# Four blocks of a second matrix asked for on GpSimd's queue, a hand order over a second norm, and two gates ahead of a late split

## The chip, the cores and the metric

The kernel runs on one core of one Trainium2 chip. Its engines are TensorE (PE in the rows, its weight loads PEld), VectorE (DVE), ScalarE (ACT), GpSimd (POOL) and SyncE (SP); each works through its own instructions in order, and DMA transfers are issued on a queue of SyncE or of GpSimd. The metric is the device time of one execution in microseconds, as the median of several runs. Where a time is given with two decimals and no unit, it is microseconds from the start of the profiled span.

## The reference

A decoder of two layers over 512 tokens of width 1024, in float32. Layer 0 mixes by pooling, layer 1 by a gated unit (SGU); both have an MLP of width 4096 behind it. Every matrix is applied in float32 accuracy.

```python
def sgu_mixer(h, w_in, ln_g, ln_b, w_s, b_s, w_out):
    z = jax.nn.gelu(h @ w_in, approximate=False)
    u, v = jnp.split(z, 2, axis=-1)
    v = layernorm(v, ln_g, ln_b)
    ...
    mixed = jnp.einsum('hts,bnshc->bnthc', ws, v) + b_s.T[None, None, :, :, None]
    gated = u * mixed.reshape(B_, S_, SGU_WIDTH)
    return gated @ w_out

def sq_relu_mlp(h, w1, w2):
    return jnp.square(jax.nn.relu(h @ w1)) @ w2

for i in range(DEPTH):
    mod = c_act @ ada_w[i] + ada_b[i]
    sh1, sc1, g1, sh2, sc2, g2 = jnp.split(mod, 6, axis=-1)
    h = modulate(rmsnorm(x, norm_mix_g[i]), sh1, sc1)
    y = pool_mixer(...) if i == 0 else sgu_mixer(...)
    x = x + g1[:, None, :] * y
    h = modulate(rmsnorm(x, norm_mlp_g[i]), sh2, sc2)
    x = x + g2[:, None, :] * sq_relu_mlp(h, mlp_w1[i], mlp_w2[i])
return rmsnorm(x, final_g)
```

## The kernel before, in words

**Products.** A float32 product is made of three products of rounded halves (`mm3`): a weight is split into `wh` (ScalarE, L199, in the SGU L1245) and `wl`, the rest (VectorE, L200, L1251), an activation into `hb` or `o` in the same way (L678, L679; L1399, L1403). So each block of 128 by 1024 weights passes ScalarE and then VectorE before TensorE can use it, and there are a few buffers for the split pairs.

**Units.** The big matrices are multiplied by a scheme with seven products of block sums in place of eight, after Strassen. A unit carries the number m of its product, in the order 1, 5, 6, then 3, 7, 2 and last 4. For m = 1, 5, 6, 4 the weight sums are made in memory, in one tile for each block: it holds the block of one product, is split, and then a DMA on GpSimd's queue adds the next block onto it (`accum_op=ALU.add`; L953 for M2, L820 for M1, L1281 for the SGU's `u`). So each such add waits for the low split (VectorE) of the product before, and the next split waits for the add. M1 is the first matrix of the MLP, M2 the second: its units (c, m) have c = 0 to 3. M2's `bt` tiles serve m = 1, 5, 6, 4, its `b` tiles m = 3 and 7; `b_load` fills the `b` tiles of c = 0 and 1 ahead and an add then turns the blocks of m = 3 into those of m = 7.

**SGU.** `u_run(j, m)` is TensorE's part of the unit (j, m) of the SGU's `u`; `u_hi`, `u_lo` are its splits, `u_add` the adds, `u_out` the eviction of its result. (1, 7) adds onto the bank of (1, 6) once `u_out(1, 6)` has copied it, (1, 4) comes last. `mix(h)`, `gate(h)`, `low(h)` are, for head h, the product with the spatial weights, the product with `u` and its high half, and the low half.

**Second norm.** Layer 1's MLP begins with a norm of the residual `x`, whose token tiles 0 and 1 make the first half and tiles 2 and 3 the second. Each tile's residual is added (VectorE, L1102, L1103), its squares are summed (ScalarE, L1113), the root is taken (VectorE L1126, then a power on GpSimd, L1127), `xs` is the scaled tile (L1153), and TensorE transposes it (`px`, L1166). `spill` writes a pair of tiles of `x` to memory (`xd`, L270), after which their buffer takes loads of MLP blocks, `raws` among them (L805).

**Order.** TensorE's order is always written by hand. VectorE, ScalarE, SyncE and GpSimd follow the hand order in some stretches (the SGU and the first half of the second norm among them); elsewhere a scheduler orders them at compile time by priority and by its own due times. `tc.keep_in_program_order` pins one instruction where it is written.

Of the kernel before, what the change touches and what calls it, by code (L numbers as in the profile page):

```python
# [14 lines left out]
P = 128  # L15
D = 1024
# [71 lines left out]
def decoder_kernel(ctx: ExitStack, tc: tile.TileContext, xtok, vecs, rows, fgrow, ada0, adag, ada1, pool_w, w1s, w1f, w1b, w2, w_v, w_u, w_o, wsT, wsN, lnp, bs, out):  # L88
# [624 lines left out]
    def mlp(i, extra, units, final):  # L713
# [105 lines left out]
        def more_of(u, o, r, n):  # L819
            G.dma_start(o, w1b[i, 2 * u[0] + u[1], r, n], accum_op=ALU.add)  # L820

        def s_sum(u):
            c, j, m = u
            if m in (5, 6) and u not in summed:
                summed.add(u)
                t = blk(c, j, 0, 0)
                if (i, m) == (1, 5) and c < 2:
                    more_of(u, t, *CHAIN[m])
                else:
                    V.tensor_tensor(t, t, blk(c, j, *CHAIN[m]), ALU.add)  # L830
                if m == 5:
                    more_of(u, blk(c, j, 0, 1), 1, 1)
# [84 lines left out]
        def b_load(c):  # L917
            t = slot(XT[c % 2], [P, 2, D], "b")
            b2[c] = [t[:, q] for q in range(2)]
            for q in range(2):  # L920
                nc.sync.dma_start(b2[c][q], piece(c, 1, 1, q))
# [271 lines left out]
    def p_units(*sums):  # L1193

        us = [("p", (c, m)) for m in (1, 5, 6) for c in range(4)]
        us += [("p", u) for u in ((0, 3), (1, 3), (1, 2), (0, 7), (1, 7), (2, 3), (3, 3), (2, 2), (2, 7), (3, 7), (3, 2))]
        us.insert(5, ("p", (0, 2)))
        after(us, ("p", (1, 6)), ("bl", (0,)), ("bl", (1,)))
        us += [("p", (c, 4)) for c in range(4)]
        after(us, ("p", (2, 2)), ("xl", (0,)))  # L1200
        after(us, ("p", (2, 7)), ("xl", (1,)))
        after(us, ("p", (3, 7)), ("sum", (0, 1)), ("sum", (1, 1)))
        for at, t, dh in sums:
            after(us, ("p", at), ("sum", (t, dh)))
        return us
# [314 lines left out]
    us += p_units(((3, 2), 0, 0), ((3, 2), 1, 0), ((1, 4), 2, 1), ((1, 4), 3, 1))  # L1520
# [149 lines left out]
    u_hi(1, 5)  # L1670
    u_run(0, 3)
    u_lo(1, 5)
    u_add(ub[0][:, 1], 1, 1, 1)
# [3 lines left out]
    u_lo(0, 4)  # L1677
    u_hi(1, 2)
    gate(2)
    gate(3)  # L1680
    u_run(1, 1)
# [4 lines left out]
    u_hi(1, 6)  # L1686
    u_lo(1, 2)
    u_lo(1, 6)
    u_run(0, 4)
    u_hi(1, 3)  # L1690
    column(24)
    gate(0)
    gate(1)
    low(0)
    low(1)
    for q in (28, 29):
        c_load(q, f"T2{q % 2}")
# [93 lines left out]
    v1 = sm.tile([P, 2], F32, name="rv", tag="rv2")  # L1791
    r1 = sm.tile([P, 2], F32, name="rr", tag="rr2")
    xs_ = slot("R0", [P, 2, D], "xs")

    def root(q):
        s = sums[0][0][:, q]
        V.scalar_tensor_tensor(v1[:, q : q + 1], s[:, 0:1], RMS_EPS, s[:, 1:2], ALU.add, ALU.add)
        G.tensor_tensor(r1[:, q : q + 1], v1[:, q : q + 1], mhalf[:, 0:1], ALU.pow)

    def first_half():  # L1800
        h32[:] = [slot(f"P{j}", [P, 4, S], "h32") for j in range(2)]
        h_[:] = hparts(["S0", "S1", "S2", "S3"])
        for k in range(0, KD, 2):
            turn_cols(0, k, (xs_[:, 0], xs_[:, 1]))
        for ks in ((0, 2), (4, 6)):
            for k in ks:
                modulate(0, k, 1)
            for k in ks:
                hi(tts[k])
            for k in ks:  # L1810
                lo(tts[k])

    for t in range(NT):
        pos[t] = bank("po", xz)
        for n, k in enumerate(ks_):
            if (t, n) == (3, 2):
                first_half()
                by[0].__exit__(None, None, None)
                spill(0)
            mm3(pos[t], cut(gt[k], ALL, tok[t]), cut(w_["o", 1, k // 2], ALL, slice(S * (k % 2), S * (k % 2) + S)), k == 2, k == 5)  # L1820
        with tc.high_priority():
            gated(t, S, S, pos[t])
        if t == 0:
            root(0)
            columns_(38)
            A.activation(xs_[:, 0], X(0), AF.Copy, scale=r1[:, 0:1])
        elif t == 1:
            root(1)
            columns_(39)
            sums.pop(0)  # L1830
            A.activation(xs_[:, 1, 0:S], X(1)[:, 0:S], AF.Copy, scale=r1[:, 1:2])
            V.tensor_scalar(xs_[:, 1, S:D], X(1)[:, S:D], r1[:, 1:2], None, ALU.mult)
# [54 lines left out]
    halves_ = normed_parts(1, 1, 1, None, True)  # L1887

    def second():
        with tc.high_priority():  # L1890
            next(halves_)
        spill(1)

    def second_too():
        with tc.high_priority():
            next(halves_, None)
# [92 lines left out]
```

## Time and profile before

| | |
|---|---|
| time, median of 3 runs | 834.9 us (834.65 to 835.15) |
| the profiled execution | 834.98 us, with a span of 833.3 us |
| mean granted clock of TensorE | 0.994 |
| TensorE busy | 820.6 us, 98% of the span |
| VectorE, ScalarE, GpSimd busy | 83%, 63%, 14% |
| moved by DMA | 194.94 MB, mean 234 GB/s |

The span is the time from the first to the last recorded instruction of the profiled execution; 1.7 us lie around it. The busy shares are averages over stages in which different things are awaited.

### The profile page before, as it was taken

To read this page: it belongs to the slowest core of one execution; us is meant where nothing else is said; L and a number is where in the kernel's file an instruction comes from. 1 tells how busy PE (TensorE), PEld (TensorE's weight loads), DVE (VectorE), ACT (ScalarE), POOL (GpSimd) and SP (SyncE) were. 2 spreads that over 40 slices of the span, in tenths; PEclk is the share of its full clock that TensorE was granted. 3 is DMA by queue.
4 is the path that set the end of the run, shared out by engine and by line. 5 is a ranking of instruction groups with operands and counts; after the bars stand their busy time and mean duration, and the time that the engine had idled before them with its cause. 6 is when DMAs were issued, how large, how long until landed. Compare 5 with 4: busy or idle time off the path is not lost.

```text
span 833.3 us, 13029 instructions
## 1 busy us (share of the span) xinstructions
PE 820.6 (98%) x5012; PEld 729.6 (88%) x5012; DVE 693.1 (83%) x885; ACT 526.2 (63%) x759; POOL 120.1 (14%) x149
## 2 busy tenths in 40 slices
PE   9999999999999999999999999999999999999996
PEld 6878899999888888888899889999999988888885
DVE  6999999998789868798979887795887578976887
ACT  3286787866756655667565436886766776655662
POOL 3010010000223210000311003101001032321000
PEclk8999999999999999999999999999999999999999
DMA  9999879999999989365797899965887699998502
GB/s 358 407 369 334 301 160 289 282 285 267 278 227 191 207 231 249 122 227 199 228 250 184 271 301 300 258 182 123 253 255 205 199 218 242 190 214 228 170 7 95
DMA packets 53620, 194.94 MB, mean 234 GB/s; under 512 B 6163, under 2 KB 6323, under 8 KB 52534
## 3 DMA queue, kind: packets, MB, share of 16 engines
q1 hardware_dynamic: 37296, 133.98, 44.4%
q0 software_dynamic: 15968, 59.79, 37.2%
q8 instruction: 39, 0.64, 0.3%
q10 hardware_dynamic: 294, 0.34, 0.1%
q14 instruction: 23, 0.19, 0.1%
HBM read 187.79 MB, written 6.31 MB: 233 GB/s over the span
## 4 chain that ended last, share of the span: by engine, by line
PE 62%; DVE 17%; DMA 12%; ACT 4%; issue 4%; POOL 1%; POOLq 0%; ACTq 0%; DVEq 0%; SPq 0%
PE pm L996 27%; PE po L212 7%; DMA ada<-in_ada 6%; DVE wl L200 4%; PE b305q L996 2%; PE b315q L996 2%; DMA bt<-in_w 2%; PE b211q L212 2%; ACT wh L199 2%; PE b311q L212 1%; PE b111q L212 1%; PE b101q L212 1%; PE b301q L212 1%; PE b201q L212 1%; DVE ada L424 1%
## 5 line engine op out<-in xcount | busy, mean ns | idle before, releaser
L996 PE MATMUL pm<-wh,o 128*128 128x512 f32 x736 | 182.5, 390 | 0.6 <-DVE o L679 0.6
L996 PEld LDWEIGHTS pm<-wh,o 128*128 128x128 f32 x736 | 137.7, 188 | 29.6 <-DVE o L679 1.1
L996 PE MATMUL pm<-wl,o 128*128 128x512 f32 x368 | 98.4, 389 | 0.0
L199 ACT ACTIVATE wh<-bt 128x1024 fp32r<-128x1024 f32 x62 | 64.8, 1058 | 45.0 <-PE pm L996 33.6
L200 DVE TENSOR_TENSOR wl<-bt,wh 128x1024 fp32r<-128x1024 f32 x62 | 75.1, 1219 | 15.3 <-ACT wh L199 15.2
L996 PEld LDWEIGHTS pm<-wl,o 128*128 128x128 f32 x368 | 69.1, 188 | 14.4
L679 DVE TENSOR_TENSOR o<-g,o 128x1024 fp32r<-128x1024 f32 x55 | 67.0, 1218 | 6.2 <-ACT o L678 6.2
L678 ACT ACTIVATE o<-g 128x1024 fp32r<-128x1024 f32 x55 | 57.5, 1047 | 10.1 <-PE pm L996 7.2
L199 ACT ACTIVATE wh<-b 128x1024 fp32r<-128x1024 f32 x32 | 34.0, 1063 | 37.6 <-PE pm L996 31.4
L953 POOL DMA_DIRECT2D bt<-in_w x48 | 41.8, 900 | 107.4 <-DVE wl L200 103.7
L200 DVE TENSOR_TENSOR wl<-b,wh 128x1024 fp32r<-128x1024 f32 x32 | 39.2, 1224 | 21.3 <-ACT wh L199 21.3
L212 PE MATMUL po<-hb,wh 128*128 128x256 f32 (+1 forms) x176 | 41.7, 329 | 0.0
L735 ACT ACTIVATE g<-g 128x512 f32<-128x512 f32 (+1 forms) x72 | 40.5, 579 | 1.1
L212 PE MATMUL po<-wh,gt 128*128 128x512 f32 x128 | 40.7, 395 | 0.0
L212 PE MATMUL po<-wh,hb 128*128 128x512 f32 x128 | 40.7, 396 | 0.0
L236 DVE SCALAR_TENSOR_TENSOR ada<-ada,cb 128x1024 f32<-128x1024 f32 x32 | 39.0, 1218 | 0.7 <-DMA ada<-in_ada 0.7
L1113 ACT ACTIVATE tmp<-x 128x512 f32<-128x512 f32 (+1 forms) x24 | 14.9, 621 | 31.9 <-DVE x L1103 31.8
L212 PEld LDWEIGHTS po<-hb,wh 128*128 128x128 f32 x176 | 29.7, 188 | 3.2
L199 ACT ACTIVATE wh<-raw 128x1024 fp32r<-128x1024 f32 x19 | 20.2, 1062 | 16.6 <-PE pm L996 13.5
L200 DVE TENSOR_TENSOR wl<-raw,wh 128x1024 fp32r<-128x1024 f32 x19 | 23.1, 1220 | 8.8 <-ACT wh L199 8.8
L1265 DVE SCALAR_TENSOR_TENSOR ada<-ada,cb 128x1024 f32<-128x1024 f32 x24 | 29.1, 1217 | 1.6 <-DMA ada<-in_ada 1.6
L212 PE MATMUL po<-hb,wl 128*128 128x256 f32 (+1 forms) x88 | 29.2, 332 | 0.0
(532 smaller groups left out, 2281.4 us busy)
## 6 DMA issues: line engine op xcount, KB each, us to landing
ada<-in_ada SPq DMA_DIRECT2D x74, 512.0 KB, 5.5
bt<-in_w POOLq DMA_DIRECT2D x48, 512.0 KB, 10.4
bt<-in_w SPq DMA_DIRECT2D x16, 512.0 KB, 6.3
raw<-in_w SPq DMA_DIRECT2D x16, 512.0 KB, 7.0
b<-in_w SPq DMA_DIRECT2D x16, 512.0 KB, 4.8
b<-in_w POOLq DMA_DIRECT2D x16, 512.0 KB, 10.2
wh<-in_ada SPq DMA_DIRECT2D x8, 512.0 KB, 9.4
wl<-in_ada SPq DMA_DIRECT2D x8, 512.0 KB, 10.0
```

The costliest lines, as they stand in the source:

```text
L199: A.activation(h[:, c], r[:, c], AF.Copy)
L200: V.tensor_tensor(l[:, c], r[:, c], f32(h[:, c]), ALU.subtract)
L212: T.matmul(o[:, c], a, b[:, c], start=first and q == 0 and not c.start, stop=last and q == 2 and c.stop is None, **kw)
L236: keep(V.scalar_tensor_tensor(r, r, 1.0, cb, ALU.mult, ALU.mult, accum_out=pmv[i, b][:, j : j + 1]))
L424: V.scalar_tensor_tensor(r, r, 1.0, cb, ALU.mult, ALU.mult, accum_out=out)
L678: A.activation(o[0], a, AF.Copy)
L679: V.tensor_tensor(o[1], a, f32(o[0]), ALU.subtract)
L735: A.activation(t, t, AF.Square)
L953: G.dma_start(r, piece(c, *nxt, q), accum_op=ALU.add)
L996: T.matmul(banks[hf], o[a][:, 2 * q + p, hf], w[q][b][:, S * p : S * p + S], start=start and q + n + p == 0, stop=stop and q + n + p == 4, ...
L1113: A.activation(tmp, xt, AF.Square, scale=D**-0.5, accum_out=o)
L1265: V.scalar_tensor_tensor(r, r, 1.0, cb, ALU.mult, ALU.mult, accum_out=pm[:, n : n + 1])
```

## The change

There are three parts. TensorE's order of instructions is the same in both kernels; only the other engines' and the queues' order differs.

In **layer 0's M2**, the four plain loads of the `b` tiles for c = 0 and 1 leave SyncE's queue for GpSimd's, and they are pinned in program order, behind unit (1, 5). One add of M1 (layer 1, first block column, m = 5) is pinned in program order too.

In **layer 1's second norm**, the second half was a generator that the scheduler ordered (`normed_parts`). Now its steps are written into the hand order: `residual`, `square_`, `root` and `scaled` of tile 2 between the steps of the first half, and those of tile 3 after it. `xs` of tile 3 is made in two halves, one by ScalarE and one by VectorE. `spill(0)` is written earlier, `spill(1)` at the end; the hand order ends only then.

In the **SGU's u blocks**, the splits of (1, 5), and with them the add that makes (1, 6), stand behind `gate(2)` and `gate(3)`; those of (1, 6) behind `gate(0)`, `gate(1)`, `low(0)` and `low(1)`; the high split of (1, 3) is last.

```diff
-                    more_of(u, blk(c, j, 0, 1), 1, 1)
+                    o = blk(c, j, 0, 1)
+                    if (i, c) == (1, 0):
+                        tc.keep_in_program_order(more_of(u, o, 1, 1))
+                    else:
+                        more_of(u, o, 1, 1)
 
         def s_prep(u):
...
             for q in range(2):
-                nc.sync.dma_start(b2[c][q], piece(c, 1, 1, q))
+                if i == 0 and c < 2:
+                    tc.keep_in_program_order(G.dma_start(b2[c][q], piece(c, 1, 1, q)))
+                else:
+                    nc.sync.dma_start(b2[c][q], piece(c, 1, 1, q))
 
...
-    def p_units(*sums):
+    def p_units(*sums, at_b=(1, 6)):
 
         us = [("p", (c, m)) for m in (1, 5, 6) for c in range(4)]
         us += [("p", u) for u in ((0, 3), (1, 3), (1, 2), (0, 7), (1, 7), (2, 3), (3, 3), (2, 2), (2, 7), (3, 7), (3, 2))]
         us.insert(5, ("p", (0, 2)))
-        after(us, ("p", (1, 6)), ("bl", (0,)), ("bl", (1,)))
+        after(us, ("p", at_b), ("bl", (0,)), ("bl", (1,)))
         us += [("p", (c, 4)) for c in range(4)]
...
     mix(2)
-    u_hi(1, 5)
     u_run(0, 3)
-    u_lo(1, 5)
-    u_add(ub[0][:, 1], 1, 1, 1)
     mix(3)
     u_hi(0, 4)
     u_run(0, 7)
     u_lo(0, 4)
+    u_hi(1, 5)
     u_hi(1, 2)
     gate(2)
     gate(3)
+    u_lo(1, 5)
+    u_add(ub[0][:, 1], 1, 1, 1)
     u_run(1, 1)
     mix(0)
     low(2)
     mix(1)
     low(3)
-    u_hi(1, 6)
     u_lo(1, 2)
-    u_lo(1, 6)
     u_run(0, 4)
-    u_hi(1, 3)
     column(24)
     gate(0)
     gate(1)
+    u_hi(1, 6)
     low(0)
     low(1)
+    u_lo(1, 6)
+    u_hi(1, 3)
...
-    v1 = sm.tile([P, 2], F32, name="rv", tag="rv2")
-    r1 = sm.tile([P, 2], F32, name="rr", tag="rr2")
-    xs_ = slot("R0", [P, 2, D], "xs")
-
-    def root(q):
-        s = sums[0][0][:, q]
-        V.scalar_tensor_tensor(v1[:, q : q + 1], s[:, 0:1], RMS_EPS, s[:, 1:2], ALU.add, ALU.add)
-        G.tensor_tensor(r1[:, q : q + 1], v1[:, q : q + 1], mhalf[:, 0:1], ALU.pow)
+    v1 = sm.tile([P, NT], F32, name="v1", tag="v1")
+    r1 = sm.tile([P, NT], F32, name="r1", tag="r1n")
+    x1 = {}
+
+    def root(t):
+        s = sums[t // 2][0][:, t % 2]
+        V.scalar_tensor_tensor(v1[:, t : t + 1], s[:, 0:1], RMS_EPS, s[:, 1:2], ALU.add, ALU.add)
+        G.tensor_tensor(r1[:, t : t + 1], v1[:, t : t + 1], mhalf[:, 0:1], ALU.pow)
+
+    def scaled(t, parts_=1):
+        h = t // 2
+        if h not in x1:
+            x1[h] = slot(f"R{h}", [P, 2, D], "xs")
+        o, r = x1[h][:, t % 2], r1[:, t : t + 1]
+        c = D // parts_
+        A.activation(o[:, 0:c], X(t)[:, 0:c], AF.Copy, scale=r)
+        if parts_ == 2:
+            V.tensor_scalar(o[:, c:D], X(t)[:, c:D], r, None, ALU.mult)
+
+    sq_ = {}
+
+    def residual(t):
+        sq_[t] = gated(t, S, S, pos[t], None, True)
+
+    def square_(t):
+        pair, cs = sums[t // 2]
+        s, cs = pair[:, t % 2], cs[t % 2]
+        cs.append(S)
+        tmp = sm.tile([P, S], F32, name="tmp", tag="tmp", bufs=2)
+        A.activation(tmp, X(t)[:, S:D], AF.Square, scale=D**-0.5, accum_out=s[:, len(cs) - 1 : len(cs)])
 
     def first_half():
         h32[:] = [slot(f"P{j}", [P, 4, S], "h32") for j in range(2)]
         h_[:] = hparts(["S0", "S1", "S2", "S3"])
         for k in range(0, KD, 2):
-            turn_cols(0, k, (xs_[:, 0], xs_[:, 1]))
+            turn_cols(0, k, (x1[0][:, 0], x1[0][:, 1]))
         for ks in ((0, 2), (4, 6)):
             for k in ks:
                 modulate(0, k, 1)
             for k in ks:
                 hi(tts[k])
+            if ks[0]:
+                square_(2)
+                root(2)
             for k in ks:
                 lo(tts[k])
+        scaled(2)
...
             if (t, n) == (3, 2):
                 first_half()
-                by[0].__exit__(None, None, None)
-                spill(0)
             mm3(pos[t], cut(gt[k], ALL, tok[t]), cut(w_["o", 1, k // 2], ALL, slice(S * (k % 2), S * (k % 2) + S)), k == 2, k == 5)
         with tc.high_priority():
-            gated(t, S, S, pos[t])
+            residual(t)
         if t == 0:
+            square_(0)
             root(0)
             columns_(38)
-            A.activation(xs_[:, 0], X(0), AF.Copy, scale=r1[:, 0:1])
+            scaled(0)
         elif t == 1:
+            spill(0)
+            square_(1)
             root(1)
             columns_(39)
-            sums.pop(0)
-            A.activation(xs_[:, 1, 0:S], X(1)[:, 0:S], AF.Copy, scale=r1[:, 1:2])
-            V.tensor_scalar(xs_[:, 1, S:D], X(1)[:, S:D], r1[:, 1:2], None, ALU.mult)
+            scaled(1, 2)
+        elif t == 3:
+            with tc.high_priority():
+                square_(3)
+                root(3)
+                scaled(3, 2)
+                spill(1)
+            by[0].__exit__(None, None, None)
+            sums.clear()
+
+    def second_half(ks):
+        for k in ks:
+            px = bank("px")
+            for q in range(2):
+                for r in range(2):
+                    T.transpose(px[:, 256 * q + P * r : 256 * q + P * r + P], x1[1][:, r, P * (k + q) : P * (k + q) + P], ident)
+            for q in range(2):
+                A.activation(h32[k // 4][:, k % 4 + q, 256:512], px[:, 256 * q : 256 * q + 256], AF.Identity, bias=mod(1, c_sh(1, k + q)), scale=scl[1][1][:, k + q : k + q + 1])
...
-    halves_ = normed_parts(1, 1, 1, None, True)
-
     def second():
         with tc.high_priority():
-            next(halves_)
-        spill(1)
+            second_half((0, 2))
 
     def second_too():
         with tc.high_priority():
-            next(halves_, None)
+            second_half((4, 6))
 
     us = [("cl", (0,)), ("cl", (1,))] + s_units(0, 0, (1,)) + s_units(0, 1, (1,)) + s_units(0, 0, (2,)) + [("x", second)] + s_units(0, 1, (2,)) + [("x", second_too), ("a", (0,))] + s_units(1, 0, (1,)) + [("a", (1,)), ("x", h_late)] + s_units(1, 1, (1,)) + s_units(1, 0, (2,)) + [("a", (2,))] + s_units(1, 1, (2,)) + [("a", (3,))]
```

GpSimd's instructions in layer 0's M2 (`bt` and `b` with L953 are the adds; `gb` is a row spread over the partitions), before:

```order
L953 DMA bt<-in_w 128x1024 x16
L261 DMA gain_2696<-line 8x128
L953 DMA bt<-in_w 128x1024
L263 DMA gb<-gain_2696 128x1024
L953 DMA bt<-in_w 128x1024 x7
L953 DMA b<-in_w 128x1024 x8
```

and after the change:

```order
L960 DMA bt<-in_w 128x1024 x16
L261 DMA gain_2696<-line 8x128
L960 DMA bt<-in_w 128x1024
L263 DMA gb<-gain_2696 128x1024
L926 DMA b<-in_w 128x1024 x4
L960 DMA bt<-in_w 128x1024 x7
L960 DMA b<-in_w 128x1024 x8
```

The four plain loads `b` of L926 stand behind `gb` and ahead of the last seven `bt` adds and the eight `b` adds.

ScalarE's instructions in the SGU, from the eviction of unit (0, 5) to that of (1, 6) (`wh<-ur` and `wh<-raw` are high splits of u blocks, `gt` the gates; the last `u<-po` is the eviction of (1, 6)), before:

```order
L1322 ACTIVATE u05q<-po 128x512
L1245 ACTIVATE wh<-ur 128x1024
L1328 ACTIVATE u<-po 128x2x256
L1245 ACTIVATE wh<-ur 128x1024
L1349 ACTIVATE gt<-u 128x512 x2
L1326 ACTIVATE u<-u15q 128x2x256
L1245 ACTIVATE wh<-ur 128x1024
L1328 ACTIVATE u<-u05q 128x2x256
L1245 ACTIVATE wh<-ur 128x1024
L1326 ACTIVATE u<-po 128x2x256
```

and after:

```order
L1329 ACTIVATE u05q<-po 128x512
L1335 ACTIVATE u<-po 128x2x256
L1356 ACTIVATE gt<-u 128x512 x2
L1252 ACTIVATE wh<-ur 128x1024 x2
L1333 ACTIVATE u<-u15q 128x2x256
L1252 ACTIVATE wh<-ur 128x1024
L1335 ACTIVATE u<-u05q 128x2x256
L1252 ACTIVATE wh<-ur 128x1024
L1333 ACTIVATE u<-po 128x2x256
```

The high split of (1, 6) stood ahead of the eviction `u<-po` of L1328; now it is the first of the two behind the second pair of gates. The one ahead of the last `u<-po` splits (1, 4) in both.

ScalarE's instructions in the second norm, from the high split of `raw0010q` to `xs` of tile 3 (`h`, `hb` are the first half's results and their high halves, `tmp,sums` the squares, `g` MLP evictions), before:

```order
L199 ACTIVATE wh<-raw0010q 128x1024
L1153 ACTIVATE xs<-x_3299,rr 128x1024
L1420 ACTIVATE h_4863<-px,mods_89,scl_93 128x256 x2
L1399 ACTIVATE hb<-h_4863 128x2x256 x2
L199 ACTIVATE wh<-raws 128x1024
L1113 ACTIVATE tmp,sums<-x_3299 128x512
L880 ACTIVATE g<-b001q 128x512
L199 ACTIVATE wh<-ch10q 128x1024
L199 ACTIVATE wh<-ch11q 128x1024
L1153 ACTIVATE xs<-x_3299,rr 128x1024
```

and after:

```order
L199 ACTIVATE wh<-raw0010q 128x1024
L1427 ACTIVATE h_4866<-px,mods_89,scl_93 128x256
L199 ACTIVATE wh<-raws 128x1024
L1427 ACTIVATE h_4866<-px,mods_89,scl_93 128x256
L1406 ACTIVATE hb<-h_4866 128x2x256 x2
L1827 ACTIVATE tmp,sums<-x_3299 128x512
L199 ACTIVATE wh<-ch10q 128x1024
L884 ACTIVATE g<-b001q 128x512
L1813 ACTIVATE xs<-x_3299,r_4755 128x1024
L199 ACTIVATE wh<-ch11q 128x1024
L1827 ACTIVATE tmp,sums<-x_3299 128x512
L882 ACTIVATE b012q<-b011q 128x512
```

The split of `raws` stood behind the two last `hb` and `xs` of tile 2, and now stands between the two last `h`; `xs` of tile 2 comes behind the split of `ch10q`. `xs` of tile 3 is two rows further on, behind another split.

## Rows read from the trace of the kernel before

**Rows 1.** The page, busy time of each engine: us, share of the span, instructions.

```profile
PE 820.6 (98%) x5012; PEld 729.6 (88%) x5012; DVE 693.1 (83%) x885; ACT 526.2 (63%) x759; POOL 120.1 (14%) x149
```

**Rows 2.** Windows of 20 us: length, busy us and instructions per engine, clock.

```profile
440.00:460.00 20.00, 20.00 (x176) 20.00 (x175) 19.24 (x28) 11.37 (x16) 0.86 (x1) 1.00 0.79 209
500.00:520.00 20.00, 20.00 (x130) 17.94 (x129) 14.50 (x28) 13.64 (x23) 6.53 (x9) 1.00 1.01 302
```

**Rows 3.** Waits of TensorE: us in total, times, longest; nine entries in all.

```profile
PE pc L348 <- DVE edge L313: 1.1, 1, 1.1
...
PE pm L996 <- DVE o L679: 0.6, 1, 0.6
...
PE px L1166 <- ACT xs L1153: 0.5, 1, 0.5
```

**Rows 4.** Timelines of PE, SP and ACT, 216 to 230: start us, us, instruction.

```profile
229.08 1.20 PE L996 MATMUL pm<-wh,o 128*128 128x512 f32 x4 [0.63 <-DVE o L679]
...
216.30 2.21 SPq L921 DMA_DIRECT2D b<-in_w  x4
...
222.16 3.90 ACT L199 ACTIVATE wh<-bt 128x1024 fp32r<-128x1024 f32 x4 [1.33 <-DMA bt<-in_w]
```

**Rows 5.** Timelines of POOL and ACT, DMA issues 265 to 290 and 298 to 304.

```profile
265.23 0.56 POOL L263 DMA_DIRECT2D gb<-gain  x1 [5.86 <-DMA gain<-line]
265.78 3.61 POOL L953 DMA_DIRECT2D bt<-in_w  x4
...
276.73 1.06 ACT L199 ACTIVATE wh<-b 128x1024 fp32r<-128x1024 f32 x1 [1.65 <-PE pm L996]
...
293.05 1.06 ACT L199 ACTIVATE wh<-b 128x1024 fp32r<-128x1024 f32 x1 [1.51 <-PE pm L996]
...
bt<-in_w POOLq DMA_DIRECT2D x7, 512.0 KB, 12.4
b<-in_w POOLq DMA_DIRECT2D x4, 512.0 KB, 11.9
...
b<-in_w SPq DMA_DIRECT2D x4, 512.0 KB, 4.1
```

**Rows 6.** Timelines of POOL, DVE, ACT, PE, SP, 437 to 459; `ur` transfers.

```profile
447.68 0.86 POOL L1281 DMA_DIRECT2D ur<-in_w_u  x1 [8.01 <-DVE wl L1251]
...
445.82 1.21 DVE L1251 TENSOR_TENSOR wl<-ur,wh 128x1024 fp32r<-128x1024 f32 x1
...
449.48 1.29 DVE L1352 TENSOR_TENSOR gt<-u,gt 128x512 fp32r<-128x512 f32 x2
...
455.06 0.60 ACT L1326 ACTIVATE u<-po 128x512 f32<-128x512 f32 x1
...
452.04 0.37 PE L212 MATMUL po<-as,wl 128*128 128x256 f32 x1
...
458.57 0.28 PE L212 MATMUL po<-hb,wl 128*128 128x256 f32 x1
...
451.65 3.56 SPq L185 DMA_DIRECT2D raw<-in_w_o  x3
...
DMA to landing us min/median/max: 4.0/6.0/8.1
```

**Rows 7.** Timelines of SP, ACT, PE, POOL, 508 to 522; `raws` transfers.

```profile
508.25 0.94 SPq L805 DMA_DIRECT2D raws<-in_w1b  x2
...
516.42 1.05 ACT L199 ACTIVATE wh<-raws 128x1024 fp32r<-128x1024 f32 x1
...
521.55 0.98 PE L1166 MATMUL px<-ident,xs 128*128 128x128 f32 x7 [0.51 <-ACT xs L1153]
...
519.22 0.57 POOL L1127 TENSOR_TENSOR rr<-rv,mhalf 128x1 f32<-128x1 f32 x1 [0.99 <-DVE rv L1126]
521.31 0.89 POOL L820 DMA_DIRECT2D ch10q<-in_w1b  x1 [1.52 <-PE b002q L212]
...
DMA to landing us min/median/max: 6.1/7.0/7.3
```

More of the change, by code (lines that the diff above doesn't have):

```diff
@@ L819, in more_of @@
         def more_of(u, o, r, n):
-            G.dma_start(o, w1b[i, 2 * u[0] + u[1], r, n], accum_op=ALU.add)
+            return G.dma_start(o, w1b[i, 2 * u[0] + u[1], r, n], accum_op=ALU.add)
         def s_sum(u):
@@ L1519, in decoder_kernel @@
     after(us, ("s", (3, 1, 3)), ("tl", (0,)))
-    us += p_units(((3, 2), 0, 0), ((3, 2), 1, 0), ((1, 4), 2, 1), ((1, 4), 3, 1))
+    us += p_units(((3, 2), 0, 0), ((3, 2), 1, 0), ((1, 4), 2, 1), ((1, 4), 3, 1), at_b=(1, 5))
     rr = []
```

## The prediction

> **What bounds the kernel now.** I began with the busy times of the page [rows 1]: TensorE is busy 820.6 of 833.3 us. The busy time by stretches [rows 2] says the same of two of the stretches in which the change works: 20.00 of 20.00 us, while VectorE and ScalarE are each below that. The granted clock there is 1.00, so no time can come from the clock. Two things follow. TensorE has no idle time in which it could catch up: whatever it waits is added to the end, wherever it happens. And the change can win only what TensorE waits for today. So the third view was the list of TensorE's waits [rows 3]. The list has nine entries, none over 1.1 us, and two of them lie where the change works: 0.6 us for the low half of a block sum (`o`, L679), 0.63 in the bracket of the matmuls at 229.08 [rows 4], and 0.5 us for `xs` of the second norm (L1153), 0.51 at 521.55 [rows 7]. The two make 1.14; matmuls overlap a little, so I allow 1.5 us as the most that the change can win. What it can lose has no such bound. So the work that remained was to replay, instruction by instruction, the three places in the new order with the durations of the trace.
>
> The profiled execution took 834.98 us with a span of 833.3, 1.7 us lying around it; it is 0.08 above the median, so sums made against it hold for the median too.
>
> **Part 1, the four blocks of layer 0's M2.** Before, SyncE issues them in 2.21 us from 216.30, straight behind a `bt` load [rows 4]. ScalarE waits 1.33 us for that load until 222.16 and then makes four `wh` in 3.90 us; VectorE's `wl` follow, then the block sum that TensorE waits for. On one queue the four stand behind that `bt`, so taking them away speeds it up by nothing or, if they share the transfer engines with it, by up to the whole wait of 0.63. I take 0.3: the queue's order speaks for little.
>
> After, GpSimd issues them behind `gb<-gain`, which goes out at 265.23 after a wait of 5.86 us [rows 5]. Four issues at 0.9 (3.61 for four, same rows) put them on the queue from 265.8 to 268.5. The `bt` accumulates that stand there now land at a median of 12.4 us, and `gb` itself in 5.6. So the first block lands between 270.9, right behind `gb`, and 278.2, and the last by 280.9. ScalarE reads them, `wh<-b`, at 276.73, 279.45, 282.17 and 284.89, each time held by TensorE and not by the transfer [rows 5]. Only the first can be late, by 1.5 us, and a unit of 24 matmuls (5.4 us) lies between the split and TensorE's use. So: nothing. The seven `bt` and eight `b` accumulates behind them start about 3.6 us later. The `b` accumulates take 11.9 us, and the first, issued at 279.35, is read by ScalarE at 293.05, again held by TensorE: 279.35 + 3.6 + 11.9 = 294.9. That is 1.8 us late at a ScalarE that idles 1.51 us there, for a block which TensorE takes up a unit or two later. I take nothing here too, and if the cover is gone, 1 to 5 us. The sum for this part is −0.3.
>
> [...]
>
> **Part 3, the u blocks.** The block of (1,5) is split, then GpSimd adds onto it to make (1,6), whose split comes before the next add, which makes (1,4). Before, the adds go out at 437.92 and 447.68 and the splits run at 443.26 (ScalarE, held by the transfer) and 445.82 (VectorE) [rows 6]. The change puts the low split of (1,5) behind the gates of heads 2 and 3, at 440.22 + 1.28 = 441.5, and the low split of (1,6) behind `low(0)`, `low(1)`. Nothing in front of those two `low` has become longer (one `wl` of 1.22 us came into the stretch, one left), so they end, as before, between 449.48 + 1.29 = 450.8 and a little earlier; I reckon 450.3. The `wl` takes 1.21: it ends at 451.5. TensorE needs (1,6) at 452.04 [rows 6], so there it just fits. The add for (1,4) follows 0.3 to 0.65 us after its `wl` (447.68 − 445.82 − 1.21 = 0.65), at about 452.0 instead of 447.68. It lands 4.0 to 8.1 us later, the least and the most of the adds in this stretch, median 6.0 [rows 6]. That is 456.0 to 460.1. ScalarE works in order: `wh` of (1,4), which now waits for this, stands ahead of the eviction of (1,6) (`u<-po`, at 455.06 before). TensorE's (1,7), due at 458.57, adds onto the bank that this eviction empties. So TensorE waits until landing + 1.06 + 0.60 = 457.7 to 461.8: nothing to 3.2 us. At the median it would be 459.7, a wait of 1.1. But SyncE issues loads into the time of this transfer (three from 451.65 on, same rows), so I take the slow half of the range, 7.0: 452.0 + 7.0 + 1.66 − 458.57 = 2.1. The `wl` of (1,4) and what stands behind it on VectorE is late next, perhaps 0.3 at (1,4) itself: 2.4 in all. Nothing can be won here, since TensorE is busy all of 440 to 460 [rows 2].
>
> [...]
>
> **Part 2, the second half's second norm.** Before, ScalarE ran tile 2's `xs`, then the two `hb`, and only then the split of the first `raws` block, at 516.42 [rows 7]. `raws` is a load that SyncE issues at 508.25, when the spilled `x` has left the buffer; the four loads of this name took 6.1 to 7.3 us. So it lands at 514.4 to 515.5. In the new order the split `wh<-raws` stands ahead of the last `h` piece, of the two last `hb` and of the whole of the norm, on ScalarE; and the low split of `raws` stands ahead of the root on VectorE. All of it now waits for that load. The replay, from a landing at 514.4:
> - `wh<-raws` 1.05, to 515.4; the h piece 0.5, to 515.9; two `hb` 1.14, to 517.0; the square of tile 2 0.62, to 517.6.
> - VectorE: low `hb` to 518.9; the two halves of the residual of tile 3 (0.69 each) around the `wl` of `ch10q` (1.22), to 521.3.
> - The square of tile 3, 0.62 and 0.19, to 522.1, beside VectorE's `wl<-ch11q` to 522.6; the root's sum 0.15, to 522.7.
> - GpSimd issues the adds for `ch10q` and `ch11q` (0.89 each, [rows 7]) ahead of the root's power; the second cannot go before that `wl`, so it is done at 523.8; the power 0.57 (once it took 1.69), to 524.4 (525.5).
> - The last `xs`, now halved between ScalarE and VectorE, about 0.7: 525.1 (526.2). The other durations of this list are those that the same operations have before, between 506 and 523.
>
> TensorE's transposes wait for it: 525.1 instead of 521.55, so +3.6; a landing at 515.5 and a slow power make it +5.8. Halving `xs` saves 0.4 of 1.14, which is in the sum. If the first `raws` lands as early as 512.2, two us sooner than any, +1.9 is left. If the load holds nothing at all, this place costs about nothing, and wins up to 0.7. The spill of tile pair 1 comes about 7 us later than 517.63; the `raws` loads which wait for it are read far later, so I cost that at nothing, at most 1.
>
> **The sum.** 834.98 − 0.3 + 2.4 + 3.6 = 840.7; I say 840.6.
>
> **The rivals.**
> A. The forecast: both waits appear. 837 to 843.5.
> B. Only the norm's wait appears, the add of (1,4) being quick (6 us or less after an early issue): 834.98 − 0.3 + 3.6 = 838.3, from 836.5 to 840. For it: the median of 6.0. Against: SyncE's loads beside it.
> C. Only the u blocks wait, `raws` landing before ScalarE comes to its split: 834.98 − 0.3 + 2.4 = 837.1, from 835.2 to 838.5. It decides at a landing before about 511.5; the four loads say otherwise.
> D. GpSimd's blocks come late in layer 0: 1 to 5 us on top of A, up to 846. It decides where the first block lands after 278 or the later accumulates take over 14 us.
> E. Neither new wait appears: 834 to 835.8, about 834.7.
> F. The other side: the late split frees VectorE and ScalarE for the norm, the wait at 521.55 goes, and the one at 229.08 too: 834.98 − 1.5 = 833.5, at the best 833.1. It decides where `raws` lands by 511.5 and the last `xs` is done by 520.8. That each wait is half a us, which little would cover, speaks for it; the order on ScalarE against it.
>
> **How the numbers follow.** A 0.56, B 0.15, C 0.07, D 0.04, E 0.11, F 0.07. The likeliest is A at 840.6. A measurement of this kernel tells about 0.2% (1.7 us) from no change: 833.2 and 836.6 are the bounds. Faster is F's better half and a little of E, 0.05; same is the rest of E and F and the lower parts of B and C, 0.17; slower is 0.78. Of the range, 834.6 leaves out F and the lower half of E, 0.12, and 843.2 the slow end of A and D, 0.07. The likeliest case's own range is 837 to 843.5.
>
> **What would show it.** Right: in the changed trace TensorE's list of waits has a new entry at the transposes of the second norm of 3 to 6 us, released by ScalarE's or VectorE's `xs`; ScalarE idles before `wh<-raws` and names that transfer; at (1,7) a wait for ScalarE's eviction, with ScalarE idle before `wh<-ur` for an `ur` transfer; the wait at 229 is nearly the same. Wrong: TensorE's list is as before, or the entries stand at the units of M2 between 276 and 310. The prediction falls above all if the first `raws` lands before 512, or if the adds of `ur` take under 5 us.

## The result and the profile after

The changed kernel takes 843.91 us (median of 5 runs, 842.17 to 849.81) against 835.15 us for the kernel before (5 runs): a ratio of 1.011, with a 95% interval from 1.007 to 1.015. It is slower by 8.8 us where 5.7 were forecast, and 0.7 us above the end of the range. The profiled execution took 844.67 us, 9.7 us more than that of before. Three executions stand apart (1935.66 us in e1_part1 and 1662.56 in a run of before, both at a clock of 1.00, and 1019.54 us at 0.754 in e4_parts12); the times and ratios below leave them out, and the trace of parts one and two together, which is the last of them, is not read. From the page of the changed kernel, its head and the busy times, which answer to [rows 1]:

```profile
span 843.0 us, 13032 instructions
...
PE 824.9 (98%) x5012; PEld 733.7 (87%) x5012; DVE 693.3 (82%) x886; ACT 526.5 (62%) x759; POOL 123.3 (15%) x153
```

TensorE is busy 4.3 us longer than before, although it has the same 5012 matmuls. So not all of the loss is waiting; some matmuls became longer. TensorE's list of waits, against [rows 3]:

```profile
PE po L212 <- ACT u L1333: 4.3, 1, 4.3
PE px L1879 <- ACT xs L1813: 1.7, 1, 1.7
...
PE pm L1003 <- DVE o L679: 0.8, 1, 0.8
```

The first entry is new. The second is the wait at the norm's transposes, 1.2 us longer than before. The third is the block sum of M2, which was to get shorter and did not. I take the three places in turn.

**The u blocks.** Timelines of GpSimd, ScalarE and TensorE, in that order, where [rows 6] were read:

```profile
453.45 0.86 POOL L1288 DMA_DIRECT2D ur<-in_w_u  x1 [6.25 <-DVE wl L1258]
...
462.96 1.06 ACT L1252 ACTIVATE wh<-ur 128x1024 fp32r<-128x1024 f32 x1 [6.54 <-DMA ur<-in_w_u]
463.93 0.58 ACT L1333 ACTIVATE u<-po 128x512 f32<-128x512 f32 x1
...
464.56 0.58 PE L212 MATMUL po<-hb,wl 128*128 128x256 f32 x1 [4.30 <-ACT u L1333]
...
469.85 0.41 PE L1346 MATMUL po<-wsbs,v 128*128 128x128 f32 x2
```

The same place on TensorE in the kernel before, behind the 24 matmuls of (1,7) that begin at 458.57 in [rows 6]:

```profile
461.40 1.05 PE L1339 MATMUL po<-wsbs,v 128*128 128x128 f32 x8
```

The issues of DMA between 453.2 and 454.0, with the median us to landing:

```profile
ur<-in_w_u POOLq DMA_DIRECT2D x1, 512.0 KB, 9.5
```

The reader follows the chain from the top. The add for (1,4) goes out at 453.45 and lands 9.5 us later, at 462.94. ScalarE stood 6.54 us before the high split of (1,4) until then. Behind the split stands the eviction of (1,6), at 463.93, and at 464.56 TensorE's (1,7) begins, after 4.30 us. That is the predicted chain, link by link; the landing is outside the 4.0 to 8.1 us that were taken for it. Then comes what the prediction lacked. The unit (1,7) runs from 464.56 to 469.85, 5.29 us; before, the same 24 matmuls took 2.83, from 458.57 to 461.40. TensorE's windows of 2 us show why (window, its length, busy us and instructions of PE, granted clock, DMA share, GB/s):

```profile
461.00:463.00 2.00, 0.00 (x0) 1.00 0.96 324
463.00:465.00 2.00, 0.44 (x2) 0.52 0.07 27
465.00:467.00 2.00, 2.00 (x11) 0.50 0.00 0
...
469.00:471.00 2.00, 2.00 (x14) 0.78 0.86 233
```

The granted clock is still 1.00 while TensorE stands still between 461 and 463, and 0.50 in the matmuls with which it resumes. So this place costs the wait of 4.3 us and then 5.29 − 2.83 = 2.5 us.

**The second norm.** Timelines of GpSimd and ScalarE, where [rows 7] were read:

```profile
518.26 0.89 POOL L820 DMA_DIRECT2D raw<-in_w1b  x1 [6.69 <-DVE wl L200]
...
519.40 1.57 POOL L820 DMA_DIRECT2D raw<-in_w1b  x1
...
528.53 0.86 POOL L820 DMA_DIRECT2D ch11q<-in_w1b  x1 [0.84 <-DVE v L1804]
529.10 1.94 POOL L1805 TENSOR_TENSOR r<-v,mhalf 128x1 f32<-128x1 f32 x1
...
520.20 1.06 ACT L199 ACTIVATE wh<-raws 128x1024 fp32r<-128x1024 f32 x1
...
531.06 0.72 ACT L1813 ACTIVATE xs<-x,r 128x512 f32<-128x512 f32 x1 [1.69 <-POOL r L1805]
```

The transfers of `raws`, least, median and most us to landing:

```profile
DMA to landing us min/median/max: 3.5/4.2/4.9
```

ScalarE splits the first `raws` block at 520.20 with no wait: the two loads landed in 3.5 and 4.9 us, where 6.1 to 7.3 were counted. It was close, since the first had landed at 520.12. What is left of the predicted chain is its end. The root's power on GpSimd stands behind the issue of the add for `ch11q` and takes 1.94 us at 529.10, and ScalarE's `xs` waits 1.69 us for it until 531.06.

**M2.** Timelines of GpSimd and ScalarE, where [rows 5] were read:

```profile
265.49 2.14 POOL L926 DMA_DIRECT2D b<-in_w  x4
...
277.97 1.06 ACT L199 ACTIVATE wh<-b 128x1024 fp32r<-128x1024 f32 x1 [1.65 <-PE pm L1003]
...
296.27 1.06 ACT L199 ACTIVATE wh<-b 128x1024 fp32r<-128x1024 f32 x1 [3.50 <-DMA b<-in_w]
```

The four loads are issued in 2.14 us and the first is split at 277.97, held by TensorE as before. The adds behind them do come late: ScalarE waits 3.50 us for the first of their blocks, to 296.27. The four `b` adds issued between 280 and 289.5 take longer than before (11.9 in [rows 5]):

```profile
b<-in_w POOLq DMA_DIRECT2D x4, 512.0 KB, 14.9
```

TensorE waits for none of it.

Summed against before: 4.3 + 2.5 at the u blocks, 1.2 at the norm, 0.2 at the block sum, 8.2 us of the 9.7 by which the spans differ. Of the rest, 0.9 us is not the change's: at 210, ahead of its first effect, the same matmul was already that much later than before (210.49 against 209.60), and in the runs below that point stood on either side of before by a us and more. The last 0.6 us is spread over the trace and has no place here. The 0.2 at the block sum may be scatter too: in the ten traces that lack part one this wait runs from too little to be listed up to 0.8 us.

### The profile page after: what moved, and what is told of

Read it like the earlier page. It is cut to its first block, busy times and chain, and to the rows that moved or that the text cites. A ratio compares the mean times of both kernels' runs of the same rounds, so it can differ in the third digit from the quotient of the medians.

```text
span 843.0 us, 13032 instructions
## 1 busy us (share of the span) xinstructions
PE 824.9 (98%) x5012; PEld 733.7 (87%) x5012; DVE 693.3 (82%) x886; ACT 526.5 (62%) x759; POOL 123.3 (15%) x153
## 5 line engine op out<-in xcount | busy, mean ns | idle before, releaser
L212 PE MATMUL po<-hb,wh 128*128 128x256 f32 (+1 forms) x176 | 44.1, 343 | 0.0
L212 PEld LDWEIGHTS po<-hb,wh 128*128 128x128 f32 x176 | 31.7, 202 | 3.2
L1120 ACT ACTIVATE tmp<-x 128x512 f32<-128x512 f32 (+1 forms) x20 | 12.4, 620 | 29.0 <-DVE x L1110 28.9
```

Source lines behind the costliest of these rows:

```text
L212: T.matmul(o[:, c], a, b[:, c], start=first and q == 0 and not c.start, stop=last and q == 2 and c.stop is None, **kw)
L1120: A.activation(tmp, xt, AF.Square, scale=D**-0.5, accum_out=o)
```

## The experiments

The theory after the result: the three parts act each at its own place and add up; the third carries most, by one late add, ScalarE's order behind it and the half clock after it; the norm cost little because `raws` landed early. The rivals are named with each run. Ratios are to runs of before on the same chip (medians of 835.98 us for the first four runs, 836.37 for the next four and 836.00 for the last four), and one of them is good to about 0.002. What is read from a trace is one execution.

**The parts alone.** The three parts of the diff above, each alone, and the first two together.

> The kernel before with the first part alone: layer 0's four b loads on GpSimd's queue. Theory (each part costs what TensorE waits at its own place): TensorE lost 0.35 us at the block sum of M2 near 230 in the changed kernel and nothing from there to 438, so this run takes the time of before plus 0 to 0.5 us, and the wait at 229 is still there. Rival (late b blocks slow M2): plus 1 to 5 us, with waits of TensorE between 276 and 310.

> The kernel before with the second part alone: the hand order over the second half's second norm, and the pinned add. Theory (the wait at the transposes is what the order on GpSimd and ScalarE makes, whatever came before): before plus 1.3 to 1.8 us, a wait for xs of 1.5 to 2 us, raws landing 3 to 5 us after its issue. Rival (raws landed early in the changed kernel only because the late u blocks had moved the other transfers; alone it lands after 6 to 7 us and holds ScalarE, as the prediction had it): before plus 3 to 5 us.

> The kernel before with the third part alone: the later splits of the u blocks (1,5) and (1,6). Theory: before plus 5 to 8 us, of which a wait of 3 to 5 us for ScalarE's eviction of (1,6) and some 2.5 us in the matmuls right behind it, which run at the half clock. Rival (the wait is 1 to 2 us as predicted and the rest in the changed kernel came from other parts): plus 1 to 3 us and no stretch at the half clock.

> The changed kernel with the third part undone (parts one and two together). Theory (the parts add up): before plus 1.3 to 2.3 us. Rival (the norm's order costs its full 3.6 us once the u blocks no longer shift it): plus 3 to 5 us.

| run | parts | time, us | ratio, 95% interval |
|---|---|---|---|
| e1_part1 | one | 837.83 | 1.0016 (0.9999 to 1.0032) |
| e2_part2 | two | 837.07 | 1.0013 (0.9990 to 1.0037) |
| e3_part3 | three | 842.52 | 1.0075 (1.0054 to 1.0097) |
| e4_parts12 | one and two | 838.74 | 1.0032 (1.0010 to 1.0054) |
| the change | all | 843.91 | 1.011 (1.007 to 1.015) |

Within their intervals the parts add up: 0.16 + 0.13 against 0.32% for the first two together, 0.32 + 0.75 against 1.1% for all. The first two together cost 2.7 us (0.8 to 4.5), which lies between their theory and their rival and does not by itself part them. Part three alone is 6.3 us slower than before. In its trace the add takes 10.4 us, the wait at (1,7) is 5.5 and the clock falls to 0.50 too:

```profile
PE po L212 <- ACT u L1326: 5.5, 1, 5.5
```

```profile
465.00:467.00 2.00, 1.09 (x5) 0.50 0.00 0
```

Part two alone is 1.1 us slower, with a wait of 1.6 at the transposes and the second `raws` block landing in 4.6 us (the trace has no landing of the first), as against 4.9 in the full change. So the late u blocks of the full change are not what let `raws` land early, and that rival falls. For part one the interval touches 1; its trace has one wait that is longer than before, 1.6 against 0.3 us at an M2 split near 346, but a run without part one (e2_part2) has 1.0 there too. Whether part one costs its 0.16% stays open.

**Why `raws` landed early.** Part two holds an edit that the prediction passed over: an add of M1 is pinned in program order. It waits for its load only, and without the pin GpSimd issued it first; with the pin it stands behind two adds that wait for VectorE. Here the pin is taken out:

```diff
-                    if (i, c) == (1, 0):
-                        tc.keep_in_program_order(more_of(u, o, 1, 1))
-                    else:
-                        more_of(u, o, 1, 1)
+                    more_of(u, o, 1, 1)
```

> Part two alone without its pin on one add of M1, so that GpSimd issues that add, which waits for a load only, ahead of the two that wait for VectorE, as before the change. Theory (the raws load lands in 3.4 to 4.6 us only because the pin holds that add back until raws has gone out; with the add beside it, it takes 6 to 7 us as in the kernel before and holds ScalarE): a wait for xs of 3 to 4.5 us at the transposes, 1.5 to 3 us more than the 1.6 of part two alone, and a time 1.5 to 3 us above it. Rival (the pin has nothing to do with the landing): raws in under 5 us, a wait of about 1.6 us and the time of part two alone.

It takes 842.41 us, a ratio of 1.0076 (1.0054 to 1.0098). Timelines of GpSimd and ScalarE in this run:

```profile
506.16 0.90 POOL L820 DMA_DIRECT2D raw<-in_w1b  x1 [1.36 <-DMA raw<-in_w1b]
511.04 0.86 POOL L820 DMA_DIRECT2D raw<-in_w1b  x1 [3.98 <-DVE hb L1403]
...
515.47 1.06 ACT L199 ACTIVATE wh<-raws 128x1024 fp32r<-128x1024 f32 x1 [3.38 <-DMA raws<-in_w1b]
```

DMA issues between 508.5 and 509.5, us to landing of the second of the two loads (that of the first is not in the trace):

```profile
raws<-in_w1b SPq DMA_DIRECT2D x2, 512.0 KB, 9.9
```

TensorE's longest wait, and a window behind it:

```profile
PE px L1872 <- ACT xs L1806: 4.5, 1, 4.5
```

```profile
528.00:530.00 2.00, 2.00 (x12) 0.50 1.07 270
```

Without the pin an add goes out at 506.16, two us ahead of `raws`, which SyncE issues from 508.60 on. The first `raws` block is there at 515.47, 6.9 us later, where it took 3.5 in the changed kernel; the second takes 9.9 us in place of 4.9. ScalarE waits 3.38 us for the first, the transposes 4.5 us, and then the clock falls to 0.50 as at the u blocks. So the predicted chain exists, and nearly in its size: 6.1 to 7.3 us were forecast for the load, and 3.6 more than the 0.51 of before for the transposes. It was the pin that took the load out of that add's company, and that is worth 0.0076 − 0.0013, some 5 us (2.5 to 8), more than the 1.5 to 3 expected, with the clock at 0.50 here too. In the changed kernel the first of the adds is at 518.26, 1.6 us after `raws` was issued.

**What is left at the norm.** The add for `ch11q` is pinned too, which puts it behind the root of tile 3 on GpSimd:

```diff
-                    more_of(u, t, *CHAIN[m])
+                    add = more_of(u, t, *CHAIN[m])
+                    if (c, j) == (1, 1):
+                        tc.keep_in_program_order(add)
```

> Part two alone, with the add for ch11q pinned too, so that it stands behind the root of tile 3 and behind the spill on GpSimd. Theory (what is left of the wait at the transposes is the root's power behind an add's issue on GpSimd): the wait falls from 1.6 to 0 to 0.5 us, the time by 1.2 to 1.6 us below part two alone, to that of before within 0.5 us. Rival (ScalarE's and VectorE's own order, the second raws split ahead of xs, holds it anyway): the wait stays over 1 us.

836.4 us, a ratio of 0.9995 (0.9976 to 1.0014). GpSimd's timeline and the wait that is left:

```profile
521.81 0.57 POOL L1804 TENSOR_TENSOR r<-v,mhalf 128x1 f32<-128x1 f32 x1 [0.71 <-DVE v L1803]
```

```profile
PE px L1878 <- ACT xs L1812: 0.3, 1, 0.3
```

The power now takes 0.57 us and the wait is 0.3. The issue ahead of it was the cause of what remained. The times agree with that, but their intervals (1.0013 and 0.9995, each to about 0.002) are too wide to show 1.3 us.

**Where the late add is waited for.** Part three, with the high split of (1,4) behind the eviction of (1,6):

```diff
     mix(6)
-    u_hi(1, 4)
     column(27)
...
     u_run(1, 6)
+    u_hi(1, 4)
     mix(7)
```

> Part three alone, with ScalarE's eviction of (1,6) moved ahead of the high split of (1,4). Theory (TensorE waited for an eviction that could have run at once, behind a split that waited for the late add): no wait at (1,7); the late block is now felt only at (1,4), 3.8 us further on, with 1 to 3 us for VectorE's wl, and little or no stretch at the half clock: before plus 1 to 4 us, at least 2.5 us below part three alone. Rival (the late add costs the same wherever it is waited for): before plus 6 us as part three alone.

842.67 us, a ratio of 1.0071 (1.0047 to 1.0094): nothing is won, and the theory falls here to its rival. ScalarE's and VectorE's timelines and TensorE's longest wait:

```profile
456.51 0.60 ACT L1326 ACTIVATE u<-po 128x512 f32<-128x512 f32 x1 [0.28 <-PE po L212]
...
465.65 1.23 DVE L1251 TENSOR_TENSOR wl<-ur,wh 128x1024 fp32r<-128x1024 f32 x1 [6.79 <-ACT wh L1245]
...
469.67 0.68 DVE L1330 TENSOR_TENSOR u<-u,po 128x512 f32<-128x512 f32 x1
```

```profile
PE po L212 <- DVE u L1330: 6.5, 1, 6.5
```

The eviction runs at 456.51 and (1,7) does not wait. But VectorE stands 6.79 us before the low split of (1,4), and behind it, in its own order, are the subtractions (L1330) of (1,3) and (1,7), whose banks TensorE needs next. TensorE waits 6.5 us one unit later, and the clock falls there, to 0.50 in the windows from 467 to 475.

**What the half clock is worth.** Part three, with `mix(7)` moved behind (1,3) and its eight matmuls repeated five times there:

```diff
-    mix(7)
     u_lo(1, 4)
...
     u_run(1, 3)
+    for _ in range(5):
+        for t in range(NT):
+            T.matmul(four[2][:, tok[t]], vt[t][:, 1, P * 3 : P * 3 + P], wb[0][:, 7], start=True, stop=True)
+    mix(7)
```

> Part three alone, with mix(7) moved from ahead of (1,3) to behind it and its 8 matmuls made five times more on the same data into the same bank, about 5 us of TensorE's work where it waits for the eviction of (1,6); the repeats change no value. Theory (about 2.3 us of part three are matmuls at the half clock because TensorE stood still for 4 to 5.5 us): the granted clock stays at 1.00 behind the wait, and the time is 1.5 to 2.5 us below part three alone, though nothing lands sooner. Rival (the slow matmuls have another cause, a late operand or the transfers): they are as slow as in part three alone and the time is the same or longer.

842.59 us, a ratio of 1.0072 (1.0046 to 1.0098). A window where part three ran at 0.50, and the waits between 450 and 475:

```profile
465.00:467.00 2.00, 1.62 (x15) 1.00 0.00 0
```

```profile
PE po L212 <- DVE u L1330: 0.9, 1, 0.9
PE po L212 <- ACT u L1326: 0.4, 1, 0.4
```

TensorE waits 0.4 us here in place of 5.5 and the clock stays at 1.00, so the fall was due to TensorE's standing still and to nothing in the matmuls. What that is worth is less clear. The add lands as late as in part three (464.21 against 464.30), and (1,7) begins 1.6 us behind the landing in both. Its matmuls take 5.12 us in part three and 2.93 here, 2.2 less. But from the landing to the start of (1,4) it is 7.67 us in part three (to 471.97) and 6.53 here (to 470.74). So by the traces 1.1 us is saved; the rest goes to the 0.9 us that (1,4) now waits for VectorE, whose queue is as late as in part three and which the slow matmuls had covered. The medians do not show the 1.1 us (842.59 against 842.52, from ratios with intervals of about 0.0025 to either side), so the 1.5 to 2.5 expected did not come. That the clock adds to the wait is shown by the trace; the size of it in the time stays open.

**Why the add took 9.5 us.** Part three, with the three loads that SyncE issues around 452 put on GpSimd's queue behind the add:

```diff
-    load(("o", 0, 1), whole(w_o[0, 1]))
-    load(("o", 0, 0), whole(w_o[0, 0]))
-    load(("o", 0, 3), whole(w_o[0, 3]))
+    load(("o", 0, 1), whole(w_o[0, 1]), G)
+    load(("o", 0, 0), whole(w_o[0, 0]), G)
+    load(("o", 0, 3), whole(w_o[0, 3]), G)
```

> Part three alone, with the three loads of the out matrix's blocks that SyncE issued from about 452 moved to GpSimd's queue, where they stand behind the late add for (1,4). Theory (the add took 9.5 to 10.9 us because those loads shared the transfers with it, where the adds of before took 5.4 to 8.1): the add lands in 5 to 7 us, the wait at (1,7) falls from 5.5 to 0.5 to 2.5 us and with it the half-clock stretch; the loads come later and may make a new wait of 1 to 4 us where the out products begin. Rival (an add at this place is that slow by itself): it lands after 9 us or more and the wait at (1,7) stays at 4 us or more.

838.63 us, a ratio of 1.0024 (1.0003 to 1.0044). ScalarE's timeline, the add (issues between 451.4 and 452.0), TensorE's wait at (1,7) and the window behind it:

```profile
459.43 1.06 ACT L1245 ACTIVATE wh<-ur 128x1024 fp32r<-128x1024 f32 x1 [5.17 <-DMA ur<-in_w_u]
```

```profile
ur<-in_w_u POOLq DMA_DIRECT2D x1, 512.0 KB, 7.8
```

```profile
PE po L212 <- ACT u L1326: 2.8, 1, 2.8
```

```profile
461.00:463.00 2.00, 1.98 (x16) 1.00 0.57 234
```

The add lands in 7.8 us, the wait at (1,7) is 2.8 (5.5 in part three), the clock stays at 1.00 and two thirds of part three's cost are gone. 7.8 is slower than the 5 to 7 expected. Two loads of `ada` on SyncE, issued less than 3 us ahead of it, were still beside it, and the three moved loads follow it on GpSimd's queue from 452.18 on; which of them slows it no run tells apart.

**Which move makes it late.** Of part three, once only the splits of (1,6) (and the high split of (1,3)) are moved, once only those of (1,5) (of these it is the low split that comes to stand behind the gates of heads 2 and 3; the high one is later than before, but still ahead of them):

```diff
-    u_hi(1, 6)
     u_lo(1, 2)
-    u_lo(1, 6)
     u_run(0, 4)
-    u_hi(1, 3)
...
     gate(1)
+    u_hi(1, 6)
     low(0)
     low(1)
+    u_lo(1, 6)
+    u_hi(1, 3)
```

> Before, with the splits of (1,6) and the high split of (1,3) alone moved behind the gates, those of (1,5) where they were. Theory (the add for (1,4) stands behind the low split of (1,6), so this move alone makes it late): issue of that add 3 to 4 us later than before, a wait at (1,7) of 2 to 5 us and a time of before plus 2 to 6 us. Rival (both moves are needed): before within 1 us.

> Before, with the splits of (1,5) alone moved behind the gates of heads 2 and 3, those of (1,6) where they were. Theory (the add for (1,6) then lands some 5 us later, near 449, and holds ScalarE's and VectorE's order, in which the gates of heads 0 and 1 stand behind the split of (1,6)): the add for (1,4) is late by 2 to 5 us too, before plus 2 to 7 us. Rival (the add for (1,6) lands in time, and only the later place of the split of (1,6) costs): before within 1 us.

Only (1,6): 842.03 us, 1.0057 (1.0037 to 1.0077). Only (1,5): 838.10 us, 1.0018 (0.9996 to 1.0040). In the first: SyncE's first loads at this place, the add for (1,4), TensorE's wait at (1,7) and its windows behind it. Then in the second: SyncE's first loads, the add and TensorE's waits.

```profile
449.61 0.80 SPq L1256 DMA_DIRECT2D ada<-in_ada  x2
```

```profile
ur<-in_w_u POOLq DMA_DIRECT2D x1, 512.0 KB, 9.2
```

```profile
PE po L212 <- ACT u L1326: 3.8, 1, 3.8
```

```profile
461.00:463.00 2.00, 0.49 (x2) 0.85 0.15 61
463.00:465.00 2.00, 2.00 (x11) 0.50 0.00 0
```

```profile
454.70 0.80 SPq L1256 DMA_DIRECT2D ada<-in_ada  x2
```

```profile
ur<-in_w_u POOLq DMA_DIRECT2D x1, 512.0 KB, 5.5
```

```profile
PE po L212 <- DVE u L1330: 1.3, 1, 1.3
PE u15q L212 <- DVE wl L1251: 1.0, 1, 1.0
```

Both send the add out at almost the same moment (451.72 and 451.59), as part three does (453.88 in a trace that runs 1.7 us later). It takes 9.2 us in the first and 5.5 in the second. The difference is SyncE's: with (1,5) alone its loads go out from 454.70 on, behind the add, and with (1,6) alone from 449.61, ahead of it. The earlier adds on GpSimd's own queue are not what slows it: with (1,6) alone the last of them had landed at 446.32, more than 5 us before. With the quick add 1.0 and 1.3 us of waits remain; most of the rest of part three is the company in which the add travels, and the clock of 0.50 behind it. Of the two expectations the first came true; in the second the add is late as it said, but the time is 1.5 us over before (−0.3 to 3.3) where 2 to 7 were expected, and so nearer to its rival.

**Without the two costs.** Parts one and two, with the pin of e6_part2_root_first:

> The changed kernel without part three and with the add for ch11q pinned behind the root of tile 3: what would be left of the change with its two costs taken out. Theory (the first two parts then cost and win nothing): before within 0.2%. Rival (the first part costs its 0.16% as it did alone): before plus 1 to 2 us.

836.9 us, a ratio of 0.9999 (0.9980 to 1.0017), though its median lies 0.9 us over that of before. With the third part undone and the root ahead of the add, the change neither wins nor costs more than 0.2%; no version here is shown to beat the kernel before.

## Why the prediction was wrong

**Right:** the direction, and each link of part three: the add for (1,4) issued at about 452 (453.45 in a trace that runs 1.6 us later there: (1,6) begins at 453.66 in place of 452.04), the split that waits for it on ScalarE, the eviction behind it, TensorE's (1,7). Right too was that M2's four loads cover themselves, and that the later adds would be late at ScalarE and not at TensorE. Not right was which place pays most: the norm was given 3.6 us and the u blocks 2.4, and it was 1.2 and 6.8.

**The step that failed in part three is the term 7.0 for the add's landing**, in "I take the slow half of the range". It measured 9.5 in the changed kernel and 9.2 to 10.9 in the four runs where SyncE's loads were ahead of it (e3, e7, e8, e10). The range came from adds that travelled at other moments. The add for (1,4) of the kernel before, issued at 447.68, ahead of SyncE's loads, and the load on SyncE at 432.63, us to landing:

```profile
ur<-in_w_u POOLq DMA_DIRECT2D x1, 512.0 KB, 5.4
ur<-in_w_u SPq DMA_DIRECT2D x1, 512.0 KB, 4.0
```

Issued 4 us later, the same add travels among SyncE's loads, which the runs e9 to e11 show. The prediction saw three of these loads and allowed one us over the median for them; the add took four more than the 5.4 of before. The wait became 4.3 in place of 2.1. The lower end of the range, 4.0, was not an add at all: the row groups all transfers of `ur`, and the quickest is the second line. The quickest add there took 5.3.

**A term was missing:** after 4.3 us without a matmul TensorE came back at a granted clock of 0.50, and the next 24 matmuls took 2.5 us more. The prediction reads the clock of before, 1.00, and says that "no time can come from the clock"; it did not ask what a wait of some us does to it. In e8 some of it comes back as a wait for VectorE's queue, so the two are not simply added.
The clock is 0.50 behind every wait of 3.8 us or more that is shown here (3.8 in e10, 4.3 in the changed kernel, 4.5 in e5, 5.5 in e3, 6.5 in e7), and 1.00 behind the one of 2.8 (e9). Why a wait sets the clock back, and from what length on, no run shows.

**The step that failed in part two** is "the four loads of this name took 6.1 to 7.3 us. So it lands at 514.4 to 515.5". The 3.6 us for it measured 1.2. The chain itself is real, as e5 shows, where it costs 4.5 us of waiting and the clock. The first `raws` block landed in 3.5 us, at 520.12, which is 511.3 in the times of before (the trace runs 8.8 us later there). That is the prediction's own sign of being wrong, a landing before 512. What was overlooked is the smallest edit of the diff, the pin on one add, which moves that add from ahead of `raws` to behind it on another queue. For the four M2 loads the neighbours on the queue were counted, for this one add they were not.
The company counted in both places: the second `raws` block landed in 4.6 to 4.9 us with no add just ahead of it, and with one in 7.3 in the kernel before and in 9.9 in e5; the add of `ur` for (1,4) in 5.4 to 5.5 us ahead of SyncE's loads and 9.2 to 10.9 among them. How the transfers share the DMA engines no run shows.

**Part one's −0.3** came to nothing: the wait at the block sum was 0.8 with the four loads gone from SyncE (0.6 before), so nothing shows that they had slowed the `bt` load ahead of them. The lower end of its bound, nothing, was right.

**The rivals.** A came true at the u blocks, and at the norm only in the place of the wait, not in its cause. B did not come: it asked for 6 us or less for the add of (1,4), which took 9.5. Of C the premise was true, since `raws` landed before 511.5 in the times of before and did not hold ScalarE, but the root on GpSimd still made 1.2 us, and C's price for the u blocks was the same 2.4. D's second sign came, adds of over 14 us, without its cost. E and F did not come. That the sum missed by only 3 us is luck: part two was 2.4 us too dear, part three 4.4 us too cheap (2.4 against 4.3 + 2.5), and the range, which knew no half clock, ended 0.7 us too low. One step of the working does not follow either: for a landing at 512.2, which is 2.2 us before 514.4, 3.6 becomes 1.4 and not 1.9; the sum does not use it.

## What to carry to other kernels

Here a DMA's time from issue to landing belonged to the moment at which it was issued: the same add took 5.4 to 5.5 us ahead of SyncE's loads and 9.2 to 10.9 among them. When a change moves an issue, list what the other queues send around the new moment and take the price from a transfer in that company; a row that groups several transfers hides which one it was. Where TensorE is always busy, a wait of several us also asks for the clock behind it, which was 1.00 here after 2.8 us and 0.50 after 3.8. And an edit that only pins one instruction can be the one that decides beside what a load travels: the first `raws` block took 3.5 us with the pin and 6.9 without it.

## What the runs showed of the hardware that was not expected

In M2 four plain loads took 2.14 us to issue on GpSimd in the changed kernel, 0.54 each, where four adds took 3.61 in the kernel before, about 0.9 each. A power of one column on GpSimd had no one price: in the second norm of the changed kernel it took 0.57, 0.94 and 1.47 us with the engine idle before it, and 1.94 right behind the issue of an add. And after 2.8 us of standing still TensorE's clock was 1.00, after 3.8 us (only the splits of (1,6) moved) 0.50.
